# The first matrix of both MLPs by seven products for eight, with the residual kept in DRAM meanwhile

## The chip, the core and the metric

The kernel runs on one core of one Trainium2 chip. The metric is the device time of one execution in microseconds (us); smaller is better. Before the change three runs took 1334.22, 1339.44 and 1339.55 us, with a median of 1339.44 us.

## What is computed

A trunk of two layers over L = 528 tokens (16 meta tokens and 512 tokens of the sequence) with 1024 features, all in float32. Layer 0 mixes tokens by gated DeltaNet heads and windowed attention, layer 1 by dense attention. Behind each mixer stands the same MLP, and it is all that the change touches:

```python
h = h + mix
u = rmsnorm(h, mlp_norm_g[layer])
h = h + jnp.square(jax.nn.relu(u @ w_ff1[layer])) @ w_ff2[layer]   # w_ff1: 1024 x 4096, w_ff2: 4096 x 1024
```

The output is h without the meta tokens, so the mixer's output projection and the MLP of layer 1 work on 512 tokens only.

## The kernel before

Everything stands feature by token: a tile has 128 features on the partitions and the tokens in its columns. The residual is eight such tiles, `hk[0]` to `hk[7]`. A matrix product with full precision is made of three products of a reduced float type: each operand is split into a high part and the rest (`wh` and `wl` of the weights, `xh` and `xl`, or `ah` and `al`, of the activations), and `gemm` (L212) adds wh·xh, wh·xl and wl·xh into one PSUM tile for each of the feature tiles k.

Weights come in units of 1024 by 128 (512 KB). `load_unit` (L201) loads a unit on SyncE's queue into `raw`, ScalarE casts it to `wh` (L208) and VectorE makes `wl` (L209). The three tiles have two buffers each, in the pool `wp`, which is opened first and stays open to the end (L150), so the unit for the next product is prepared while the one before is multiplied, across the borders of stages too. In layer 0 a unit is multiplied with 528 tokens in two halves of 264 columns (48 matmuls); in layer 1 with 512 tokens at once (24 matmuls of 512 columns).

The stages in order: layer 0's mixer (to 348.7 us of the profile), its output projection (O0, L1079 to 1085: eight units; each result is added to the input `hr` by VectorE at L1084, and `make_x` at L1060 and L1061 multiplies with the norm's gain and splits it into `xh` and `xl`), layer 0's MLP (M0), layer 1's mixer with its output projection `c_out` (L1303), and layer 1's MLP (M1).

`mlp` (L1089) goes through the 4096 inner features in four quarters. In each quarter eight units of the first matrix give eight tiles: ScalarE takes relu out of PSUM (L1111), VectorE multiplies with PSUM for the square (L1112), ScalarE casts to `ah` (L1114), VectorE makes `al` (L1115). Then eight units of the second matrix are multiplied with these, and VectorE adds each result to the accumulator `facc` (L1133). The norm's factor is applied last, to the MLP's output: relu(c·u)² is c²·relu(u)², so only `r2` = 1/(mean square + eps) is needed. `sum_squares` (L1065) adds up the squares of `hk`; one matmul with the constant `onesd` (L1122), between the first and the second matrix of the second quarter, sums over the partitions. In the last quarter `facc` is multiplied with `r2` (L1135) and added to `hk` (L1136).

The code is recorded by Python functions; the order in which the instructions stand on each engine is set by a scheduler when the program is built. Each engine works through its own row strictly in that order and waits by semaphores for the others.

Of the kernel before, what the change touches and what calls it, by code (L numbers as in the profile page):

```python
# [17 lines left out]
P = 128  # L18
# [116 lines left out]
def build(tc, ins, out, dbg=None):  # L135
# [891 lines left out]
    ab_cm.__exit__(None, None, None)  # L1027
    psum_pool("psm0", dn=4)
# [49 lines left out]
    xs = []  # L1078
    for m in range(KT):  # L1079
# [5 lines left out]
        xs.append(make_x(m, PK_G + 8))  # L1085
# [3 lines left out]
    def mlp(layer, t0, xs, final):  # L1089
        lp_cm = tc.tile_pool(name=f"mlp{layer}", bufs=1, side="right", reuse_waits="tile")  # L1090
        lp = lp_cm.__enter__()
        acc = lp.tile([P, KT, L], F32, name="facc")
        xh, xl = [x[0] for x in xs], [x[1] for x in xs]
# [313 lines left out]
```

## Time and profile before

| | |
|---|---|
| median of three runs | 1339.44 us |
| the profiled execution's own time | 1335.85 us |
| its span, first to last instruction | 1334.1 us |
| TensorE matmul (PE) busy | 1299.1 us, 97% |
| weight loads (PEld) busy | 1180.8 us, 89% |
| VectorE (DVE), ScalarE (ACT), GpSimd (POOL) busy | 754.9, 558.6, 88.1 us |
| mean granted TensorE clock | 0.991 |
| stages, by the first product of each | O0 from 348.7, M0 from 397.9, M1 from 974.0 us |

The page is read by engine: busy time is the union of an engine's instructions, and an engine's idle time is put down to what ended it. PE's matmuls overlap each other, so how fast PE really goes is read from the distance between two starts and not from a matmul's own length.

### The profile page before, as it was taken

What the parts mean: (1) busy time and instruction counts of PE and PEld (TensorE: products, weight loads), DVE (VectorE), ACT (ScalarE), POOL (GpSimd) and SP (SyncE); (2) the same over time, 40 slices, a digit from 0 to 9 for tenths busy, and PEclk for the clock granted to TensorE, in tenths of its full rate; (3) what the DMA queues carried; (4) which work ended last, traced back from release to release, by engine and by line L of the source; (5) the groups of instructions that cost most, each with busy time, mean ns of one, the idle gap of its engine ahead of it and who ended that gap; (6) DMA issues with size and microseconds to landing.
All of it is one profiled execution on the core that took longest, in us unless ns stands there. A gap on an engine that the chain in (4) does not pass through costs nothing.

```text
span 1334.1 us, 21206 instructions
## 1 busy us (share of the span) xinstructions
PE 1299.1 (97%) x8595; PEld 1180.8 (89%) x8595; DVE 754.9 (57%) x1575; ACT 558.6 (42%) x1084; POOL 88.1 (7%) x202
## 2 busy tenths in 40 slices
PE   7998999899999999999999999999999999999998
PEld 6997999789899999999999987988788888888886
DVE  5686868986554324434335668698663244343444
ACT  4634565556533323223123357576443232231331
POOL 1051506030000000000000000000000000000000
PEclk9998999999899999999999999999999999999999
DMA  4321212100143323332332221101243333333333
GB/s 170 113 64 32 65 33 65 48 2 3 49 126 95 96 83 93 95 91 85 95 96 87 88 85 43 56 16 33 71 117 94 98 95 92 95 95 102 95 97 98
DMA packets 32081, 105.20 MB, mean 79 GB/s; under 512 B 3688, under 2 KB 3816, under 8 KB 31856
## 3 DMA queue, kind: packets, MB, share of 16 engines
q1 hardware_dynamic: 31984, 103.86, 25.9%
q8 instruction: 67, 1.10, 0.4%
q14 instruction: 30, 0.25, 0.1%
HBM read 101.73 MB, written 2.11 MB: 78 GB/s over the span
## 4 chain that ended last, share of the span: by engine, by line
PE 88%; DVE 5%; ACT 3%; POOL 2%; issue 1%; DMA 1%; SPq 0%; ACTq 0%; DVEq 0%
PE dn L219 64%; PE cq L219 5%; PE po L1292 2%; PE dn L1265 2%; PE pw L980 1%; PE pw L1286 1%; POOL u L634 1%; DVE cy L429 1%; POOL ut L633 1%; PE po L219 1%; PE rw L735 1%; PE rw L668 1%; PE rw L682 1%; PE pw L464 1%; PE rw L723 1%
## 5 line engine op out<-in xcount | busy, mean ns | idle before, releaser
L208 ACT CAST wh<-raw 128x1024 fp32r<-128x1024 f32 (+1 forms) x186 | 188.3, 1012 | 479.9 <-PE dn L219 416.7
L209 DVE TENSOR_TENSOR wl<-raw,wh 128x1024 fp32r<-128x1024 f32 (+1 forms) x186 | 219.9, 1182 | 254.0 <-ACT wh L208 249.5
L219 PE MATMUL dn<-xh,wh 128*128 128x264 f32 (+1 forms) x1184 | 297.4, 313 | 1.1 <-ACT wh L208 0.9
L219 PE MATMUL dn<-xh,wl 128*128 128x264 f32 (+1 forms) x1184 | 294.4, 312 | 0.0
L219 PE MATMUL dn<-xl,wh 128*128 128x264 f32 (+1 forms) x1184 | 294.3, 310 | 0.0
L219 PE MATMUL dn<-ah,wh 128*128 128x264 f32 (+1 forms) x896 | 232.3, 318 | 0.0
L219 PE MATMUL dn<-ah,wl 128*128 128x264 f32 (+1 forms) x896 | 230.6, 316 | 0.0
L219 PE MATMUL dn<-al,wh 128*128 128x264 f32 (+1 forms) x896 | 229.4, 314 | 0.0
L219 PEld LDWEIGHTS dn<-xl,wh 128*128 128x128 f32 x1184 | 195.7, 191 | 12.1
L219 PEld LDWEIGHTS dn<-xh,wh 128*128 128x128 f32 x1184 | 195.3, 191 | 12.4 <-issue 1.1
L219 PEld LDWEIGHTS dn<-xh,wl 128*128 128x128 f32 x1184 | 194.0, 190 | 11.1 <-issue 0.2
L219 PEld LDWEIGHTS dn<-al,wh 128*128 128x128 f32 x896 | 148.3, 189 | 11.9 <-issue 0.2
L219 PEld LDWEIGHTS dn<-ah,wh 128*128 128x128 f32 x896 | 148.0, 190 | 10.8 <-ACT ah L1051 0.3
L219 PEld LDWEIGHTS dn<-ah,wl 128*128 128x128 f32 x896 | 147.0, 188 | 11.0
L1133 DVE TENSOR_TENSOR facc<-facc,dn 128x528 f32<-128x528 f32 (+1 forms) x48 | 33.3, 693 | 129.8 <-PE dn L219 129.8
L1114 ACT CAST ah<-rl 128x528 fp32r<-128x528 f32 (+1 forms) x64 | 40.1, 627 | 89.3 <-DVE rl L1112 89.3
L1115 DVE TENSOR_TENSOR al<-rl,ah 128x528 fp32r<-128x528 f32 (+1 forms) x64 | 44.8, 701 | 43.2 <-ACT ah L1114 43.0
L1112 DVE TENSOR_TENSOR rl<-rl,dn 128x528 f32<-128x528 f32 (+1 forms) x64 | 44.1, 689 | 0.0
L429 DVE SCALAR_TENSOR_TENSOR cy<-cin,pk,cy 128x526 f32<-128x526 f32 (+1 forms) x48 | 38.2, 797 | 1.3 <-ACT cy L426 1.0
L1111 ACT ACTIVATE rl<-dn 128x528 f32<-128x528 f32 (+1 forms) x64 | 38.2, 597 | 0.0
L633 POOL TENSOR_TENSOR ut<-abc,u 128x150 f32<-128x150 f32 (+14 forms) x60 | 29.8, 497 | 93.8 <-DVE abc L625 89.5
L1224 POOL MEMSET cvt<- 128x128 f32 x2 | 0.4, 204 | 526.2 <-PE pw L457 526.2
(447 smaller groups left out, 1726.9 us busy)
## 6 DMA issues: line engine op xcount, KB each, us to landing
raw<-in_w SPq DMA_DIRECT2D x128, 512.0 KB, 3.6
raw<-in_w_in SPq DMA_DIRECT2D x22, 512.0 KB, 3.7
raw<-in_w_c SPq DMA_DIRECT2D x12, 512.0 KB, 3.6
raw<-in_w_o SPq DMA_DIRECT2D x8, 512.0 KB, 3.7
raw<-in_w_o SPq DMA_DIRECT2D x16, 256.0 KB, 2.7
gcb<-gdram SPq DMA_DIRECT2D x8, 264.0 KB, 4.5
hr<-in_h SPq DMA_DIRECT2D x8, 264.0 KB, 2.7
out<-h SPq DMA_DIRECT2D x8, 256.0 KB, 2.0
```

Of the source, the lines that this page charges most:

```text
L208: S.copy(out=wh, in_=raw)
L209: V.tensor_tensor(out=wl, in0=raw, in1=wh, op=ALU.subtract)
L219: T.matmul(o, a[:, k, :], b[k][:, sl], start=first and k == 0 and i == 0, stop=last and k == n - 1 and i == 2)
L429: V.scalar_tensor_tensor(out=y[:, a:a + n], in0=x[:, b:b + n], scalar=w(j), in1=y[:, a:a + n], op0=ALU.mult, op1=ALU.add)
L633: G.tensor_tensor(out=ut[:, :, :, :n], in0=arow, in1=ucol, op=ALU.mult)
L1111: S.activation(out=tview(rl), in_=pview(ps), func=AF.Relu)
L1112: V.tensor_tensor(out=tview(rl), in0=tview(rl), in1=pview(ps), op=ALU.mult)
L1114: S.copy(out=a[:, t0:], in_=rl[:, t0:])
L1115: V.tensor_tensor(out=b[:, t0:], in0=rl[:, t0:], in1=a[:, t0:], op=ALU.subtract)
L1133: V.tensor_tensor(out=tview(ak), in0=tview(ak), in1=pview(ps), op=ALU.add)
L1265: T.matmul(ps[:, s, :HL], a[:, sl], b[:, s * HL:(s + 1) * HL], start=i == 0, stop=i == 2)
L1292: T.matmul(po, a[:, kc, :], b, start=kc == 0 and i == 0, stop=kc == NC and i == 2)
```

## The change

The first matrix of both MLPs is multiplied by Strassen's scheme in Winograd's form. Two neighbouring units of the first matrix (two output tiles m and m+1) and the two halves of the 1024 input features make a 2 by 2 block matrix; the feature halves and the two halves of the tokens (264 or 256 columns) make the other one. The eight block products become seven, each of 4 feature tiles by 3 split parts, 12 matmuls of 264 columns in layer 0 and of 256 columns in layer 1.

- **Activations.** `Fast.add` replaces `make_x` behind O0 and `c_out`. It makes the seven operands `B11`, `B21`, `B22`, `T1` to `T4` (sums and differences of the blocks, each split into high part and rest) on ScalarE and VectorE.
- **Weights.** `weight_groups` loads two units at a time (1 MB), VectorE makes the sums of blocks in `sums` (L1226, L1228, L1230 of the new file), and each of three and a half groups a pair is split (L1201, L1202). `prepare` keeps a ring of five split groups. The second matrix goes through the same ring.
- **Products.** `pair` runs the seven products in three banks of PSUM. One of them, `pa`, is copied out by ScalarE three times and goes on accumulating each time; these copies and one of `pd` (`e0` to `e3`) are the partial sums that the outputs share. Relu, square and split follow on ScalarE and VectorE; the last product and the second tile of a pair are finished within the next pair.
- **Residual.** `facc` is gone and `hk` itself is the accumulator. The residual is written to DRAM by GpSimd's DMA queue (`park`) and read back twice (`reload`, into the two buffers of `hr`): for the sum of squares in the second quarter, and in the third quarter, where it is added.
- **Pools.** The weight pool is closed and opened again at each border of stages (`weight_pool`), in the room that other pools have left.

```diff
-    wp = ctx.enter_context(tc.tile_pool(name="wp", bufs=2, side="left"))
...
+    def weight_pool(name, bufs=2):
+        if "cm" in wpool:
+            wpool.pop("cm").__exit__(None, None, None)
+        if name is not None:
+            wpool["cm"] = tc.tile_pool(name=name, bufs=bufs, side="left", reuse_waits="tile")
+            wpool["p"] = wpool["cm"].__enter__()
+        return wpool["p"]
...
+        wp = wpool["p"]
...
+    weight_pool(None)
...
+        def add(self, k):
+            t0, n, g = self.t0, self.n, pkc(self.gcol + k)
+            m, i = t0 + n, k % 4
...
+            if k < 4:
+                x = self.temp.tile([P, L], F32, name=f"xf{k}")
+                S.activation(out=x[:, t0:], in_=hk[k][:, t0:], func=AF.Copy, scale=g)
+                self.split("B11", i, a[:, t0:m], b[:, t0:m], x[:, t0:m])
+                self.first[i] = x
+                V.tensor_tensor(out=x[:, t0:m], in0=x[:, t0:m], in1=x[:, m:], op=ALU.subtract)
+                self.split("T1", i, a[:, m:], b[:, m:], x[:, t0:m])
+                return
+            x, hs = self.first.pop(i), hk[k]
+            S.activation(out=a[:, t0:], in_=hs[:, t0:], func=AF.Copy, scale=g)
+            V.scalar_tensor_tensor(out=b[:, t0:], in0=hs[:, t0:], scalar=g, in1=a[:, t0:], op0=ALU.mult, op1=ALU.subtract)
+            self.ops["B21"][i] = (a[:, t0:m], b[:, t0:m])
+            self.ops["B22"][i] = (a[:, m:], b[:, m:])
+            t2, t3, t4 = fresh("t2"), fresh("t3"), fresh("t4")
+            V.scalar_tensor_tensor(out=t2, in0=hs[:, m:], scalar=g, in1=x[:, t0:m], op0=ALU.mult, op1=ALU.add)
+            self.split("T2", i, *part("T2"), t2, -1.0)
+            V.scalar_tensor_tensor(out=t3, in0=hs[:, m:], scalar=g, in1=x[:, m:], op0=ALU.mult, op1=ALU.subtract)
+            self.split("T3", i, *part("T3"), t3)
+            V.scalar_tensor_tensor(out=t4, in0=hs[:, t0:m], scalar=g, in1=t2, op0=ALU.mult, op1=ALU.subtract)
+            self.split("T4", i, *part("T4"), t4, -1.0)
...
-            s = pool.tile([P, L], F32, name="sqk", tag="sqk", bufs=2)
-            S.activation(out=s[:, t0:], in_=hk[k][:, t0:], func=AF.Square)
+            s = pool.tile([P, L], F32, name="sqk", tag=tags[0], bufs=2)
+            x = src(k)
+            t0 = L - x.shape[1]
+            S.activation(out=s[:, t0:], in_=x, func=AF.Square)
...
+    def park(layer, k, t0=0):
+        G.dma_start(out=hdram[layer][:, k, t0:], in_=hk[k][:, t0:])
+    fq_cm = tc.tile_pool(name="fq0", bufs=1, side="left", reuse_waits="tile")
+    fq = fq_cm.__enter__()
+    ft_cm = tc.tile_pool(name="ft0", bufs=1, side="left", reuse_waits="tile")
+    fast = Fast(fq, ft_cm.__enter__(), PK_G + 8, 0)
+    weight_pool("wo0")
...
-        xs.append(make_x(m, PK_G + 8))
+        park(0, m)
+        fast.add(m)
+    weight_pool(None)
+    ft_cm.__exit__(None, None, None)
...
+        def reload(m):
+            o = mp.tile([P, L], F32, name="hr", tag="hr", bufs=2)[:, t0:]
+            G.dma_start(out=o, in_=hdram[layer][:, m, t0:])
+            return o
+        def weight_groups():
+            def split(src):
+                k = src.shape[1]
+                wh = wp.tile([P, KT, P], F32R, name="wh", tag="wh", bufs=RING)
+                wl = wp.tile([P, KT, P], F32R, name="wl", tag="wl", bufs=RING)
+                S.copy(out=wh[:, :k], in_=src)
+                V.tensor_tensor(out=wl[:, :k], in0=src, in1=wh[:, :k], op=ALU.subtract)
...
+            todo = [(w, q * 8 + m) for q in range(4) for w in ("w1", "w2") for m in range(0, 8, 2)]
+            loaded = [load(*todo[0])]
+            for i, (w, m) in enumerate(todo):
+                if i + 1 < len(todo):
+                    loaded.append(load(*todo[i + 1]))
+                raw = loaded.pop(0)
...
+                s = wp.tile([P, 4, 4, P], F32, name="sums", tag="sums", bufs=1)
+                yield split(flat(raw[:, 0:2]))
+                wide4 = lambda t: t.rearrange("p a k m -> p a (k m)")
+                V.tensor_tensor(out=wide4(s[:, 1:3]), in0=wide4(raw)[:, 0:4:3],
+                                in1=wide4(raw[:, 2:3]).to_broadcast([P, 2, 4 * P]), op=ALU.add)
+                V.tensor_tensor(out=s[:, 3], in0=s[:, 2], in1=raw[:, 0], op=ALU.add)
+                yield split(flat(s[:, 2:4]))
+                V.tensor_tensor(out=s[:, 0], in0=s[:, 3], in1=raw[:, 1], op=ALU.add)
+                yield split(flat(s[:, 0:2]))
+                yield split(raw[:, 3])
...
+        def prepare():
+            while len(groups) < RING or len(groups) - RING in used:
+                g = next(source, None)
+                if g is None:
+                    return
+                groups.append(g)
+        def product(o, g, half, name, start):
+            wh, wl = groups[g]
+            for k in range(4):
+                xh, xl = fast.ops[name][k]
+                for i, (a, b) in enumerate(((wh, xh), (wh, xl), (wl, xh))):
+                    T.matmul(o, a[:, half * 4 + k, :], b, start=start and k == 0 and i == 0, stop=k == 3 and i == 2, skip_group_check=not start)
+        def activated(m, c):
+            S.activation(out=c[:, t0:], in_=c[:, t0:], func=AF.Square)
+            a, b = hl_tile(m, False), hl_tile(m, True)
+            S.copy(out=a[:, t0:], in_=c[:, t0:])
+            V.tensor_tensor(out=b[:, t0:], in0=c[:, t0:], in1=a[:, t0:], op=ALU.subtract)
+            return a, b
+        def pair(base, m, before):
+            ps, ps2 = ps_dense(), ps_dense()
+            pa, pb, pd = ps[:, 0, :n], ps[:, 1, :n], ps2[:, 0, :n]
+            c0 = lp.tile([P, L], F32, name="c0", tag="c0", bufs=2)
+            c1 = lp.tile([P, L], F32, name="c1", tag="c1", bufs=2)
+            lo, hi = slice(t0, t0 + n), slice(t0 + n, L)
+            e = [lp.tile([P, HL], F32, name=f"e{i}", tag=f"e{i}")[:, :n] for i in range(4)]
+            prepare()
+            product(pa, base, 0, "B11", True)
+            S.copy(out=e[0], in_=pa)
+            product(pb, base, 1, "B21", True)
+            used.add(base)
+            V.tensor_tensor(out=c0[:, lo], in0=e[0], in1=pb, op=ALU.add)
+            before()
+            prepare()
+            product(pa, base + 1, 1, "T2", False)
+            S.copy(out=e[1], in_=pa)
+            product(pd, base + 1, 0, "T1", True)
+            used.add(base + 1)
+            S.copy(out=e[2], in_=pd)
+            prepare()
+            product(pa, base + 2, 1, "T3", False)
+            S.copy(out=e[3], in_=pa)
+            V.tensor_tensor(out=c1[:, hi], in0=e[3], in1=e[2], op=ALU.add)
+            product(pd, base + 2, 0, "B22", False)
+            used.add(base + 2)
+            S.activation(out=c1[:, hi], in_=c1[:, hi], func=AF.Relu, scale=-1.0)
+            V.tensor_tensor(out=c0[:, hi], in0=e[1], in1=pd, op=ALU.add)
+            S.activation(out=c0[:, t0:], in_=c0[:, t0:], func=AF.Relu)
+            acts[m] = activated(m, c0)
+            def end():
+                prepare()
+                product(pa, base + 3, 0, "T4", False)
+                used.add(base + 3)
+                S.activation(out=c1[:, lo], in_=pa, func=AF.Relu, scale=-1.0)
+                acts[m + 1] = activated(m + 1, c1)
+            return end
         for q in range(4):
...
+            acts = {}
+            end = lambda: None
+            for m in range(0, 8, 2):
+                end = pair(base, m, end)
+                base += 4
+            end()
             if q == 1:
-                sq = sum_squares(lp, t0)
+                sq = sum_squares(lp, reload, ("c0", "c1"))
...
             for m in range(8):
+                prepare()
+                gemm(dst(ps), groups[base], ah, al)
+                used.add(base)
+                base += 1
+                ak = hk[m]
                 if q == 0:
                     S.copy(out=tview(ak), in_=pview(ps))
-                else:
+                elif q < 3:
                     V.tensor_tensor(out=tview(ak), in0=tview(ak), in1=pview(ps), op=ALU.add)
+                if q == 2:
+                    hr = reload(m)
+                    V.tensor_tensor(out=ak[:, t0:], in0=ak[:, t0:], in1=r2[:, t0:], op=ALU.mult)
+                    V.tensor_tensor(out=ak[:, t0:], in0=ak[:, t0:], in1=hr, op=ALU.add)
                 if q == 3:
-                    V.tensor_tensor(out=ak[:, t0:], in0=ak[:, t0:], in1=r2[:, t0:], op=ALU.mult)
-                    V.tensor_tensor(out=hk[m][:, t0:], in0=hk[m][:, t0:], in1=ak[:, t0:], op=ALU.add)
+                    o = lp.tile([P, L], F32, name="last", tag="c0", bufs=2)
+                    V.tensor_tensor(out=tview(o), in0=tview(r2), in1=pview(ps), op=ALU.mult)
+                    V.tensor_tensor(out=ak[:, t0:], in0=ak[:, t0:], in1=o[:, t0:], op=ALU.add)
...
+    weight_pool("wc")
...
-                xs.append(make_x(m, PK_G + 24, NM))
+                park(1, m, NM)
+                fast.add(m)
...
+    cp_cm.__exit__(None, None, None)
+    fq_cm = tc.tile_pool(name="fq1", bufs=1, side="right", reuse_waits="tile")
+    fq = fq_cm.__enter__()
+    ft_cm = tc.tile_pool(name="ft1", bufs=1, side="right", reuse_waits="tile")
+    fast = Fast(fq, ft_cm.__enter__(), PK_G + 24, NM)
     weave((c_out(4, KT), 1))
-    cp_cm.__exit__(None, None, None)
+    ft_cm.__exit__(None, None, None)
```

**TensorE at the end of the first matrix in the second quarter of layer 0.** Before, the squares' matmul (`sqa`, `onesd`) stands there as well:

```order
L219 MATMUL dn<-xh_4689,wl 128x264 x2
L219 MATMUL dn<-xh_4751,wh 128x264 x2
L219 MATMUL dn<-xl_4752,wh 128x264 x2
L219 MATMUL dn<-xh_4751,wl 128x264 x2
L1122 MATMUL dn<-sqa,onesd 128x264 x2
L219 MATMUL dn<-ah_5762,wh 128x264 x2
```

and with the change (`T4h`, `T4l` are an operand of the last product of a pair):

```order
L1250 MATMUL dn<-T4h_4782,wl 128x264
L1250 MATMUL dn<-T4h_4863,wh 128x264
L1250 MATMUL dn<-T4l_4864,wh 128x264
L1250 MATMUL dn<-T4h_4863,wl 128x264
L1313 MATMUL dn<-sqa,onesd 128x264 x2
L232 MATMUL dn<-ah_5995,wh 128x264 x2
```

The squares' matmul has kept its place: ahead of all products of the second matrix in that quarter.

**ScalarE: the squares.** Before, each of the eight squares (L1070) stands in O0, right behind the tile that it squares:

```order
L208 CAST wh<-raw 128x1024
L1060 ACTIVATE xh_4689<-h,pk 128x528
L1070 ACTIVATE sqk<-h 128x528
L208 CAST wh<-raw 128x1024
L1060 ACTIVATE xh_4751<-h,pk 128x528
L1070 ACTIVATE sqk<-h 128x528
```

With the change one square (L1143) stands in the second quarter's third pair, and seven behind its last pair, each of a tile `hr` that was read back:

```order
L1287 ACTIVATE c_6272<-c_6272 128x264
L1289 ACTIVATE c_6271<-c_6271 128x528
L1296 ACTIVATE c_6272<-dn 128x264
L1254 ACTIVATE c_6271<-c_6271 128x528
L1254 ACTIVATE c_6272<-c_6272 128x528
L1256 CAST ah_6399<-c_6271 128x528
L1256 CAST ah_6421<-c_6272 128x528
L1201 CAST wh<-raw 128x1024
L1143 ACTIVATE sqk<-hr 128x528 x7
L1201 CAST wh<-raw 128x1024 x4
```

So the seven squares have moved behind everything that the last pair asks of ScalarE.

**ScalarE at the opening of O0.** Before, the first unit's cast is not among these rows; it was made earlier:

```order
L770 ACTIVATE osb<-osb,ro 16x128
L1051 CAST ah_4227<-yA_80 128x528
L1051 CAST ah_4231<-yA_81 128x528
L1051 CAST ah_4235<-yA_82 128x528
L1051 CAST ah_4239<-yA_83 128x528
L1051 CAST ah_4243<-yB 128x528
L1051 CAST ah_4247<-yB 128x528
L1051 CAST ah_4251<-yB 128x528
L1051 CAST ah_4255<-yB 128x528
L208 CAST wh<-raw 128x1024
L1060 ACTIVATE xh_4317<-h,pk 128x528
```

With the change:

```order
L783 ACTIVATE osb<-osb,ro 16x128
L1067 CAST ah_4230<-yA_80 128x528
L1067 CAST ah_4234<-yA_81 128x528
L1067 CAST ah_4238<-yA_82 128x528
L1067 CAST ah_4242<-yA_83 128x528
L1067 CAST ah_4246<-yB 128x528
L1067 CAST ah_4250<-yB 128x528
L1067 CAST ah_4254<-yB 128x528
L1067 CAST ah_4258<-yB 128x528
L221 CAST wh<-raw 128x1024 x3
L1116 ACTIVATE xf_4332<-h,pk 128x528
```

The casts of O0's first units now all stand behind the eight casts of the mixer's outputs, three of them ahead of the first result.

## Rows read from the trace of the kernel before

**Rows 1.** The page: engines; the chain that ended last, by engine.

```profile
PE 1299.1 (97%) x8595; PEld 1180.8 (89%) x8595; DVE 754.9 (57%) x1575; ACT 558.6 (42%) x1084; POOL 88.1 (7%) x202
...
PE 88%; DVE 5%; ACT 3%; POOL 2%; issue 1%; DMA 1%; SPq 0%; ACTq 0%; DVEq 0%
```

**Rows 2.** PE's waits over the span: total, times, longest.

```profile
PE dn L297 <- ACT sqk L295: 7.3, 1, 7.3
...
PE dn L219 <- ACT wh L208: 0.9, 1, 0.9
```

**Rows 3.** Windows of the two MLPs: length, busy time by engine, granted clock, DMA.

```profile
397.80:770.00 372.20, 371.49 (x3078) 371.14 (x3077) 157.43 (x178) 114.94 (x146) 0.00 (x0) 1.00 0.31 91
974.00:1329.00 355.00, 354.96 (x1539) 288.46 (x1537) 149.16 (x172) 106.98 (x137) 0.00 (x0) 1.00 0.32 97
```

**Rows 4.** Timeline of PE, layer 0: start, length, instruction; 23 rows between.

```profile
449.95 0.40 PE L219 MATMUL dn<-ah,wh 128*128 128x264 f32 x2
...
455.74 0.40 PE L219 MATMUL dn<-ah,wh 128*128 128x264 f32 x2
```

**Rows 5.** Timeline of PE, layer 1; 26 rows between.

```profile
1039.66 0.40 PE L219 MATMUL dn<-ah,wl 128*128 128x512 f32 x1
...
1045.90 0.40 PE L219 MATMUL dn<-ah,wl 128*128 128x512 f32 x1
```

**Rows 6.** Groups of instructions, 400 to 755 us: count, busy, mean ns, idle before.

```profile
L219 PEld LDWEIGHTS dn<-xl,wh 128*128 128x128 f32 x506 | 78.5, 188 | 0.0
...
L209 DVE TENSOR_TENSOR wl<-raw,wh 128x1024 fp32r<-128x1024 f32 x62 | 75.9, 1224 | 124.9 <-ACT wh L208 120.7 <-PE dn L1122 2.5
...
L208 ACT CAST wh<-raw 128x1024 fp32r<-128x1024 f32 x61 | 64.0, 1049 | 191.0 <-PE dn L219 183.2 <-issue 7.8
L1115 DVE TENSOR_TENSOR al<-rl,ah 128x528 fp32r<-128x528 f32 x32 | 22.7, 708 | 21.8 <-ACT ah L1114 21.7
...
L1114 ACT CAST ah<-rl 128x528 fp32r<-128x528 f32 x32 | 20.3, 634 | 44.7 <-DVE rl L1112 44.7
L1111 ACT ACTIVATE rl<-dn 128x528 f32<-128x528 f32 x32 | 19.3, 604 | 0.0
```

**Rows 7.** Groups of VectorE over the span, smaller forms.

```profile
L209 DVE TENSOR_TENSOR wl<-raw,wh 128x512 fp32r<-128x512 f32 x16 | 10.9, 683 | 0.0
...
L592 DVE TENSOR_TENSOR dt<-pw,dt 128x256 f32<-128x256 f32 x16 | 6.1, 413 | 0.0
```

**Rows 8.** ScalarE out of PSUM, 264 columns: ns min/median/max.

```profile
L319 ACT COPY gt<-rw x2: 368/368/369, 23.4 to 27.2; 32x264 f32<-32x264 f32 x2
```

**Rows 9.** DMA issues: count, KB each, median us to landing.

```profile
raw<-in_w SPq DMA_DIRECT2D x128, 512.0 KB, 3.6
...
hr<-in_h SPq DMA_DIRECT2D x8, 264.0 KB, 2.7
out<-h SPq DMA_DIRECT2D x8, 256.0 KB, 2.0
...
yB<-in_h SPq DMA_DIRECT2D x4, 264.0 KB, 5.7
```

**Rows 10.** Timeline of ScalarE and PE where O0 opens.

```profile
350.20 2.23 ACT L1051 CAST ah<-yB 128x528 fp32r<-128x528 f32 x4
...
348.75 1.46 PE L219 MATMUL dn<-ah,wh 128*128 128x264 f32 x4
```

**Rows 11.** Windows of PE: length, PE busy, granted clock, DMA; three are slow stretches.

```profile
105.00:115.20 10.20, 9.23 (x43) 0.50 0.19 51
347.40:354.20 6.80, 6.75 (x27) 0.50 0.00 1
354.20:360.00 5.80, 5.80 (x49) 1.00 0.10 15
787.70:791.10 3.40, 3.40 (x18) 0.50 0.00 0
```

**Rows 12.** Timeline of PE, the longest wait of the mixer.

```profile
105.97 0.47 PE L659 MATMUL rw<-ident,U 128*128 128x128 f32 x1 [6.06 <-DVE U L646]
```

More of the change, by code (lines that the diff above doesn't have):

```diff
@@ L1047, in build @@
     hk = [h[:, k, :] for k in range(KT)]
+    hdram = [dp.tile([P, KT, L], F32, name=f"hdram{i}") for i in range(2)]
     yh, yl = [], []
@@ L1063, in make_x, with __init__, split @@
         return a, b
-    def sum_squares(pool, t0=0):
+    class Fast:
+        def __init__(self, pool, temp, gcol, t0):
+            self.pool, self.temp, self.gcol, self.t0, self.n = pool, temp, gcol, t0, (L - t0) // 2
+            self.first, self.ops = {}, {n: [None] * 4 for n in ("B11", "B21", "B22", "T1", "T2", "T3", "T4")}
+        def split(self, name, i, a, b, src, sign=1.0):
+            S.activation(out=a, in_=src, func=AF.Copy, scale=sign)
+            if sign == 1.0:
+                V.tensor_tensor(out=b, in0=src, in1=a, op=ALU.subtract)
+            else:
+                V.scalar_tensor_tensor(out=b, in0=src, scalar=sign, in1=a, op0=ALU.mult, op1=ALU.subtract)
+            self.ops[name][i] = (a, b)
+        def add(self, k):
+            t0, n, g = self.t0, self.n, pkc(self.gcol + k)
+            m, i = t0 + n, k % 4
+            a = xp.tile([P, L], F32R, name=f"xh{k}", tag=f"xh{k}")
+            b = xp.tile([P, L], F32R, name=f"xl{k}", tag=f"xl{k}")
+            fresh = lambda name: self.temp.tile([P, HL], F32, name=name, tag=name, bufs=2)[:, :n]
+            part = lambda name: [self.pool.tile([P, HL], F32R, name=f"{name}{c}{i}")[:, :n] for c in "hl"]
+            if k < 4:
[18 more added lines that the diff above has]
+            self.split("T4", i, *part("T4"), t4, -1.0)
@@ new lines, in weight_groups, with load @@
+        def weight_groups():
[5 more added lines that the diff above has]
+                V.tensor_tensor(out=wl[:, :k], in0=src, in1=wh[:, :k], op=ALU.subtract)
+                return wh, wl
+            def load(name, i):
+                raw = wp.tile([P, 4, 4, P], F32, name="raw", tag="raw", bufs=2)
+                for j in range(2):
+                    nc.sync.dma_start(out=raw[:, 2 * j:2 * j + 2].rearrange("p a k m -> p (a k) m"),
+                                      in_=ins[f"{name}_{layer}"][i + j])
+                return raw
+            flat = lambda t: t.rearrange("p a k m -> p (a k) m")
+            todo = [(w, q * 8 + m) for q in range(4) for w in ("w1", "w2") for m in range(0, 8, 2)]
[4 more added lines that the diff above has]
+                raw = loaded.pop(0)
+                if w == "w2":
+                    yield split(flat(raw[:, 0:2]))
+                    yield split(flat(raw[:, 2:4]))
+                    continue
+                s = wp.tile([P, 4, 4, P], F32, name="sums", tag="sums", bufs=1)
+                yield split(flat(raw[:, 0:2]))
+                wide4 = lambda t: t.rearrange("p a k m -> p a (k m)")
[6 more added lines that the diff above has]
+                yield split(raw[:, 3])
@@ L1141, in build @@
     xs2 = []
[L1142 removed]
+    mlp(0, 0, fast, lambda m: xs2.append(make_x(m, PK_G + 16)))
+    weight_pool(None)
+    fq_cm.__exit__(None, None, None)
     tap("h2", h)
@@ L1328, in build @@
     mark("M1")
-    mlp(1, NM, xs, lambda m: nc.sync.dma_start(out=out[m], in_=hk[m][:, NM:]))
+    mlp(1, NM, fast, lambda m: nc.sync.dma_start(out=out[m], in_=hk[m][:, NM:]))
+    weight_pool(None)
+    fq_cm.__exit__(None, None, None)
     psum_pool(None)
```

37 lines of the change are left out of this document (14 added, 23 removed).

## The prediction

> **What bounds the kernel now.** I read the page first: TensorE (PE) is busy in 97% of the span and holds 88% of the chain that ended last [rows 1], so time is saved only where PE has less to do, and lost wherever it is made to wait. Next the list of PE's waits: the longest are 7.3 us at the start and 6.1 us in layer 0's mixer, and all matmuls of L219 together waited 0.9 us for a weight cast [rows 2]. Then the two MLPs by windows: in 372.2 and 355.0 us PE is idle for less than 1 us each, while VectorE (DVE) is busy in 157.4 and 149.2 us and ScalarE (ACT) in 114.9 and 107.0 us [rows 3]. So both MLPs run at PE's pace, with more than half of each other engine free.
>
> PE's pace is read from starts. In layer 0, 48 matmuls of 264 columns lie between 449.95 and 455.74 us: 0.1206 us each [rows 4]. In layer 1, 27 matmuls of 512 columns lie between 1039.66 and 1045.90 us: 0.2311 us each [rows 5].
>
> **What PE saves.** A pair of tiles needs 84 matmuls for 96 in layer 0. Over 16 pairs that is 192 fewer at 0.1206 us, 23.2 us. In layer 1 a pair takes 84 of 256 columns for 48 of 512. No row has 256 columns with these operands; scaled from 264 columns it is 0.117 us. So 1344 at 0.117 us are 157.2 us, where 768 at 0.2311 us were 177.5: 20.3 us saved. Together **-43.5 us**.
>
> This needs each weight load to go on beside another matmul, now with 0.117 us to hide in. A load takes 188 ns [rows 6], yet layer 0 of the kernel before starts a matmul with a load of its own every 0.1206 us [rows 4], so loads overlap there already. The Trainium skill ("TensorE: Matmul & The Clock Gate", the part on packing small matmuls) says that a weight load overlaps with matmuls in flight only where the row groups differ, and these use all rows; it speaks against halving the columns of layer 1. By that rule each of the 1344 would cost its load as well, 0.188 us, and the sum would be 253 us higher; the trace disagrees, with 0.1206 us.
>
> **The squares: the largest cost.** The matmul with `onesd` stands on PE ahead of all products of the second matrix in the second quarter, before and after. Before, its eight squares had been made in O0. Now seven of them stand on ACT behind the last pair's work, and each reads a tile that GpSimd's queue brings back from DRAM into one of two buffers. From the end of the last product the chain goes: ACT's relu of 264 columns (0.37 [rows 8]), two squares (0.60 each, as the relu of 528 in [rows 6]), two casts (0.63 each), one weight cast (1.05) and the second residual's square (0.60): 4.5 us. The third tile has been loaded by then, so three rounds remain in which the other buffer is filled and squared: 3 x (L + 0.65), with L the time from issue to landing and 0.05 for the hand-overs. DVE's last sum (0.70) and its hand-over end it, 0.9. PE has nothing else in its row: it waits 7.4 + 3L.
>
> The trace has no DMA issued by GpSimd. SyncE's load of the same 264 KB lands in 2.7 us, a store in 2.0, one in a crowded queue in 5.7 [rows 9]; these are my bounds, and a faster landing is excluded by the 2.0 of a plain store. I take L = 3.5, near the 2.7, since nothing else is loading much then but GpSimd has to issue it. That gives 17.9 us (13.4 to 24.5), in both layers: **+35.8 us** (27 to 49). The Trainium skill ("DMA: Bandwidth & Descriptors", the anatomy of a DMA on the GpSimd path) gives about 2.0 us plus the bytes at 436 GB/s, an estimate of 2.6 us here; by it the two stalls would be 5.4 us shorter, and no run here shows it yet.
>
> **The openings.** With the weight pool closed at each border, no unit is ready when a stage begins.
> - O0: the first cast now stands behind eight casts which end at 352.43 us (350.20 + 2.23 [rows 10]); with its 1.05 us PE starts at 353.5 instead of 348.75. The rest `wl` of 1.22 us is half covered by the first products: **+5.2 us** (3 to 8).
> - M0: the first pair's load needs the room of `Fast`'s temporaries, so it starts after the last tile's add (0.7) and about 1.1 us of `Fast.add`; it lands in 3.6 us [rows 9] and is cast in 1.05: 6.7 us with hand-overs. Then the second group needs three sums on DVE (1.22 + 2 x 0.68 [rows 6, 7]) and a cast; the first product covers part of it, 3.5 us remain. **+10.2 us** (6.7 to 15).
> - M1: the last tiles of `c_out` have 12 matmuls (2.8 us) each, but the add and `Fast.add` cost DVE 2 x 0.71 + 6 x 0.41 [rows 6, 7], 3.9 us: four tiles lose 4.5. The opening costs M0's 10.2 less the 5.1 by which its load is free earlier, about two tiles. **+9.6 us** (5 to 15).
>
> **Inside a pair** PE has 10.1 us of matmuls. DVE has, in mean durations, 3 x 1.22 + 0.68 for the splits, 1.22 + 2 x 0.68 for the sums, 3 x 0.41 and 2 x 0.71 for the outputs: 9.6 us [rows 6, 7]. ACT has 3.5 x 1.05 for the casts, six of 264 columns at 0.37 and five of 528 at about 0.62: 9.0 us [rows 6, 8]. Back to back they overlap a little (four casts of 0.63 take 2.22 [rows 10]), so both fit, at nine tenths. I take 0.45 us lost a pair, 32 times: **+14 us** (0 to 30), nearer to nothing because the ring of five groups evens it out.
>
> **Clock.** Around 347.4 us, after a stretch in which PE was partly idle, the granted clock was 0.50 (1.2 GHz) for 6.8 us, and later for 3.4 us [rows 11]; PE did 27 matmuls in the first of them, where 49 fit into 5.8 us afterwards. Beside the mixer's 6.06 us wait [rows 12] a slow stretch lasts 10.2 us [rows 11]. Half of a slow stretch is lost: 1.7, 3.4 or up to 5.1 us. Both stalls at the squares are longer than that wait; I take 2.7 us each, between the two shorter ones. The openings of M0 and M1 may cost one more, 1.7: **+7 us** (3 to 12). **The end** loses one of two DVE steps behind the last product: -0.7.
>
> Hidden, at nothing: the parking of `h` and the third quarter's reads (DVE adds 2 x 0.7 us there to a unit of 5.8 us; cover of over 2 us, and if it went, eight waits of L at most); the larger loads (the DMA share is 0.31 [rows 3] and falls).
>
> **Sum:** -43.5 + 35.8 + 5.2 + 10.2 + 9.6 + 14 + 7 - 0.7 = +37.6 us. On the profiled execution's 1335.85 us that is 1373.5, given as **1374 us**. That execution was 3.6 us under the median of three, 1339.44. All low bounds together give 1336, all high ones 1420; the terms are independent of each other, so I take 1350 to 1400 for this case.
>
> **Rivals.**
> 1. *The squares hide* (not slower). All of the reads depend only on two buffers and on squares that ACT could make during the first matrix, whose quarter lasts over 40 us: eight reads of 3.5 us fit. If ACT were through with them 18 us before the last product, 35.8 us and some 4 of the clock go: 1334 us, 1320 to 1345 by the pairs' bounds. It is decided by the place of the seven squares on ACT, and the order shown has them last. Chance 0.07.
> 2. *DVE becomes the bound in the pairs.* DVE waited 0.68 us (21.7 in 32) before each `al` for ACT [rows 6]. If three such waits a pair are not covered, a pair takes 9.6 + 2.0 = 11.6 us, 1.5 lost instead of 0.45: 34 us more, 1408 us. It decides when DVE's row runs behind the ring. Chance 0.13.
> 3. *The scheme does not save on PE:* if a matmul cannot start sooner than 188 ns after another because of its load [rows 6], layer 1 takes 1344 x 0.188 = 252.7 instead of 157.2, and the time is 1469. Layer 0's spacing speaks against it [rows 4]. Chance 0.02.
>
> **Numbers.** The forecast has 0.78. A measurement of this kernel can tell about 0.5%, 6.7 us, from no change: 1333 to 1346. Rival 1 gives half of its chance to faster; a few hundredths of the forecast's low tail lie below 1346. Faster 0.04, same 0.06, slower 0.90. The range goes from 1347 to 1406: it leaves out rivals 1 and 3, half of rival 2 and the forecast's tails, about 0.2.
>
> **What will show it.** The first matrix of a quarter falls from 46.3 us (384 x 0.1206) to about 42.3 (336 x 0.1206, and 4 x 0.45) in layer 0, matmuls of 256 columns start every 0.117 us; PE waits near 18 us for DVE's `sqa` at L1313, twice, with the clock at 0.50 behind it; waits of some us where O0, M0 and M1 begin; a few tenths a pair. The forecast is wrong if L1313 waits under 8 us, if the pairs lose over 1 us each, or if the spacing is not 0.117 us.

## The result, and the profile after

The changed kernel takes 1380.24 us (median of four runs, 1378.83 to 1382.18), the kernel before 1336.83 us in the runs beside it. The ratio is 1.0326, with a 95% interval of 1.0293 to 1.0359: slower. The prediction was 1374 us, in a range of 1347 to 1406. The profiled execution has a span of 1377.1 us, 43.0 more than before; the sum had said 37.6.

The page of the changed kernel, the two lines that answer to [rows 1]:

```profile
PE 1288.0 (94%) x8979; PEld 1188.1 (86%) x8979; DVE 921.8 (67%) x1847; ACT 702.0 (51%) x1412; POOL 113.7 (8%) x250
...
PE 63%; issue 24%; DVE 5%; ACT 4%; POOL 2%; DMA 2%; SPq 0%; POOLq 0%; ACTq 0%; DVEq 0%
```

TensorE is busy for 11.1 us less, yet the span is longer: it waits. The list of its waits names where (the five largest new ones; compare [rows 2]; `po` is a result of `c_out`):

```profile
PE dn L1313 <- DVE sqa L1146: 33.6, 2, 16.9
PE dn L1250 <- ACT wh L1201: 10.9, 3, 6.5
...
PE dn L232 <- ACT wh L221: 4.9, 1, 4.9
PE po L232 <- DVE wl L222: 3.2, 1, 3.2
...
PE dn L1250 <- DVE wl L1202: 1.6, 3, 0.7
```

The squares' matmul alone makes 33.6 us, in two waits. How one of them is built shows in the timeline of layer 0, by engine:

```profile
548.18 0.28 PE L1250 MATMUL dn<-T4h,wl 128*128 128x264 f32 x1
565.35 2.13 PE L1313 MATMUL dn<-sqa,onesd 128*128 128x264 f32 x4 [16.88 <-DVE sqa L1146]
...
549.02 1.16 ACT L1254 ACTIVATE c<-c 128x528 f32<-128x528 f32 x2
550.08 1.15 ACT L1256 CAST ah<-c 128x528 fp32r<-128x528 f32 x2
551.14 1.04 ACT L1201 CAST wh<-raw 128x1024 fp32r<-128x1024 f32 x1
552.09 0.64 ACT L1143 ACTIVATE sqk<-hr 128x528 f32<-128x528 f32 x1
554.09 0.64 ACT L1143 ACTIVATE sqk<-hr 128x528 f32<-128x528 f32 x1 [1.36 <-DVE sqa L1146]
556.12 0.65 ACT L1143 ACTIVATE sqk<-hr 128x528 f32<-128x528 f32 x1 [1.38 <-DMA hr<-hdram]
...
563.91 0.64 ACT L1143 ACTIVATE sqk<-hr 128x528 f32<-128x528 f32 x1 [1.40 <-DMA hr<-hdram]
...
553.02 0.55 POOL L1191 DMA_DIRECT2D hr<-hdram  x1 [7.75 <-ACT sqk L1143]
```

ScalarE gets to the first of the seven squares at 552.09, after relu, squares, two casts and one weight cast. From then on a square comes every 2 us: it frees one of two buffers, GpSimd issues the next read (553.02), and its tile is squared 3.1 us later (556.12). The DMA part of the page gives the landing itself, and shows that the second layer does the same:

```profile
hr<-hdram POOLq DMA_DIRECT2D x16, 264.0 KB, 3.0
...
hr<-hdram POOLq DMA_DIRECT2D x16, 256.0 KB, 2.9
```

The clock is the next cost. Windows of TensorE: in the wait, behind it, and then; and at the openings of M0 and O0 (length, busy, granted clock, DMA share):

```profile
551.00:565.30 14.30, 0.00 (x0) 0.50 0.55 176
565.30:571.40 6.10, 6.05 (x23) 0.50 0.16 47
571.40:580.00 8.60, 8.60 (x73) 1.00 0.20 53
407.63:421.29 13.66, 8.29 (x32) 0.50 0.58 197
349.61:359.85 10.24, 4.87 (x20) 0.50 0.24 69
```

At 0.50 (1.2 GHz) the 6.1 us behind the wait do the work of three: 3.05 us lost. Behind the second wait, in layer 1, the slow stretch lasts 6.0 us, with about the same loss.

What the pairs save is read from the windows of undisturbed quarters, from the first product to the second matrix's first matmul: the last two quarters of layer 0 and of layer 1.

```profile
615.49:658.08 42.59, 42.59 (x338) 41.61 (x337) 31.26 (x41) 31.43 (x55) 0.00 (x0) 1.00 0.29 100
704.38:747.01 42.63, 42.63 (x339) 41.59 (x338) 32.49 (x43) 31.44 (x55) 0.00 (x0) 1.00 0.30 104
1200.71:1242.24 41.53, 41.53 (x338) 40.35 (x336) 30.92 (x41) 30.81 (x55) 0.00 (x0) 1.00 0.30 103
1286.42:1327.97 41.55, 41.55 (x337) 40.34 (x336) 32.12 (x43) 30.84 (x55) 0.00 (x0) 1.00 0.32 106
```

VectorE and ScalarE are busy for three quarters of the time in these windows, so neither is full. Before, the first matrix of a quarter took 384 x 0.1206 = 46.3 us in layer 0 [rows 4] and, by the starts in the trace, 44.4 us in the first two quarters of layer 1 (192 x 0.2311 [rows 5]) and 44.2 in its last two. The change gains 3.7 us a quarter in layer 0 and 2.6 to 2.8 in layer 1, about 25.6 us in eight quarters.

### The profile page after: what moved, and what is told of

Read it like the earlier page. It is cut to its first block, busy times and chain, and to the rows that moved or that the text cites. A ratio compares the mean times of both kernels' runs of the same rounds, so it can differ in the third digit from the quotient of the medians.

```text
span 1377.1 us, 22737 instructions
## 1 busy us (share of the span) xinstructions
PE 1288.0 (94%) x8979; PEld 1188.1 (86%) x8979; DVE 921.8 (67%) x1847; ACT 702.0 (51%) x1412; POOL 113.7 (8%) x250
## 4 chain that ended last, share of the span: by engine, by line
PE 63%; issue 24%; DVE 5%; ACT 4%; POOL 2%; DMA 2%; SPq 0%; POOLq 0%; ACTq 0%; DVEq 0%
PE dn L232 28%; PE dn L1250 12%; PE cq L232 5%; PE po L1495 2%; PE dn L1468 2%; DMA hr<-hdram 1%; PE pw L1489 1%; PE pw L993 1%; POOL u L647 1%; DVE cy L442 1%; PE rw L695 1%; POOL ut L646 1%; PE rw L681 1%; PE rw L748 1%; PE rw L736 1%
## 5 line engine op out<-in xcount | busy, mean ns | idle before, releaser
L1201 ACT CAST wh<-raw 128x1024 fp32r<-128x1024 f32 (+1 forms) x128 | 120.5, 943 | 201.1 <-PE dn L232 172.1
L1202 DVE TENSOR_TENSOR wl<-raw,wh 128x1024 fp32r<-128x1024 f32 (+1 forms) x128 | 139.3, 1090 | 63.9 <-ACT wh L1201 62.2
L1250 PE MATMUL dn<-xh,wh 128*128 128x264 f32 (+1 forms) x512 | 152.6, 298 | 11.7 <-ACT wh L1201 10.9
L1250 PE MATMUL dn<-xh,wl 128*128 128x264 f32 (+1 forms) x512 | 146.8, 289 | 1.6 <-DVE wl L1202 1.6
L1250 PE MATMUL dn<-xl,wh 128*128 128x264 f32 (+1 forms) x512 | 147.2, 288 | 0.0
L1250 PEld LDWEIGHTS dn<-xh,wh 128*128 128x128 f32 x512 | 99.2, 194 | 18.1 <-ACT wh L1201 12.1
L1202 DVE TENSOR_TENSOR wl<-sums,wh 128x1024 fp32r<-128x1024 f32 x64 | 78.0, 1224 | 39.4 <-ACT wh L1201 38.8
L1201 ACT CAST wh<-sums 128x1024 fp32r<-128x1024 f32 x64 | 66.8, 1050 | 72.4 <-PE dn L232 45.2
L1250 PEld LDWEIGHTS dn<-xh,wl 128*128 128x128 f32 x512 | 98.9, 194 | 2.5 <-DVE wl L1202 2.5
L1250 PEld LDWEIGHTS dn<-xl,wh 128*128 128x128 f32 x512 | 99.4, 194 | 0.1
L232 PE MATMUL dn<-xh,wh 128*128 128x264 f32 x416 | 91.5, 297 | 1.1 <-DVE last L1335 0.8
L232 PE MATMUL dn<-xl,wh 128*128 128x264 f32 x416 | 90.4, 293 | 0.0
L232 PE MATMUL dn<-xh,wl 128*128 128x264 f32 x416 | 89.2, 293 | 0.0
L222 DVE TENSOR_TENSOR wl<-raw,wh 128x1024 fp32r<-128x1024 f32 (+1 forms) x58 | 63.0, 1088 | 11.6 <-ACT wh L221 11.1
```

What stands on the lines that cost most here:

```text
L222: V.tensor_tensor(out=wl, in0=raw, in1=wh, op=ALU.subtract)
L232: T.matmul(o, a[:, k, :], b[k][:, sl], start=first and k == 0 and i == 0, stop=last and k == n - 1 and i == 2)
L1201: S.copy(out=wh[:, :k], in_=src)
L1202: V.tensor_tensor(out=wl[:, :k], in0=src, in1=wh[:, :k], op=ALU.subtract)
L1250: T.matmul(o, a[:, half * 4 + k, :], b, start=start and k == 0 and i == 0, stop=k == 3 and i == 2, skip_group_check=not start)
```

## The experiments

Each kernel ran beside the kernel before on the same chip. Ratios are to the kernel before, with 95% intervals; the changed kernel stands at 1.0326.

### 1. The squares later

```diff
-            if q == 1:
-                sq = sum_squares(lp, reload, ("c0", "c1"))
...
             for m in range(8):
                 ps = ps_dense()
...
                     final(m)
+            if q == 1:
+                sq = sum_squares(lp, reload, ("c0", "c1"))
...
```

> The squares, their sums and the matmul with onesd are recorded behind the second matrix of the second quarter instead of ahead of it; r2 is first read in the third quarter. Theory (the changed kernel loses two waits of 16.9 and 16.7 us there, and about 3 us more behind each at a granted clock of 0.50): the two waits fall under 2 us each, the slow stretches behind them go, and the time falls by about 39 us, from 1380 to 1341. Rival A (the wait itself is the whole cost, the clock costs nothing): 34 us less, 1346. Rival B (the squares only push the weight casts back on ScalarE, so the second matrix waits in their place): less than 20 us gained, over 1360, with waits on wh at the second matrix's first units.

Measured: 1342.31 us, 1.0052 (1.0037 to 1.0067), 37.9 us less than the changed kernel. The list of TensorE's waits has none at the squares' matmul any more, and the clock stays at 1.00 from 423.5 to 979.9 us. The quarter behind the moved matmul got 1.0 us longer in layer 0 and 1.3 in layer 1. So 33.6 us of waits and 2 x 3.05 of clock go, 2.3 come back: 37.4. The theory stands, 1 us off; rival B falls, and rival A, which leaves the clock out, is 4 us off.

### 2. Four buffers for the reads

```diff
-            o = mp.tile([P, L], F32, name="hr", tag="hr", bufs=2)[:, t0:]
+            p, tag = (lp, "hs") if m % 2 else (mp, "hr")
+            o = p.tile([P, L], F32, name="hr", tag=tag, bufs=2)[:, t0:]
```

> The reads of the parked residual get four buffers instead of two; nothing else is changed. Theory (the chain of the wait is made of rounds in which a buffer is squared and read again, 2 us a tile, because only two are free): with four buffers, four tiles have landed when ScalarE is through with the last pair, and the remaining three land together; each wait at the squares' matmul falls from 16.9 to about 10.5 us and the time by about 13 us, to 1367 (1362 to 1372). Rival (ScalarE's own work and GpSimd's issuing make the chain, not the number of buffers): each wait stays over 15 us and the time within 4 us of 1380.

Measured: 1369.19 us, 1.0247 (1.0223 to 1.0271), 11.1 us less. The waits in this kernel:

```profile
PE dn L1314 <- DVE sqa L1146: 23.5, 2, 11.8
```

5.1 us less each. The theory had 6.4: the additions to the sum keep ScalarE from squaring the landed tiles back to back, as in this row of its timeline:

```profile
553.67 1.18 ACT L1143 ACTIVATE sqk<-hr 128x528 f32<-128x528 f32 x2 [1.37 <-DVE sqa L1146]
```

The rounds through two buffers were a third of the wait. In layer 0 the first of the seven squares starts 3.6 us after the last product, in both kernels; from there to the end of the sum it is 8.2 us instead of 13.2.

### 3. The openings

```diff
+    unit0 = load_unit(ins["w_o0"][0])
...
+        with tc.issue_after(cast0):
+            S.copy(out=a, in_=s)
...
+        if m == 6:
+            early.append(load_pair(rawp, "w1", 0, 0))
...
+            if k1 == KT and m == 5:
+                early.append(load_pair(rawp, "w1", 1, 0))
```

`rawp` is a pool of two raw tiles, opened ahead of `Fast`'s; `cast0` is the cast of `unit0`.

> Only the openings are changed: the first unit of the output projection is cast ahead of the eight casts of the mixer's outputs, and the raw tiles of the MLP have a pool of their own, so that the first pair's load of each MLP goes out while the output projection still runs. Theory (a stage waits at its start for a load or a cast that comes late): O0's wait of 4.9 us goes, of M0's 6.5, 0.6 and 1.1 us some 3 to 4 go, and M1's opening gets 2 to 4 us shorter; with the clock behind them 8 to 20 us less, about 1368. Rival (the openings wait for the operands that Fast.add makes of the last tile, whatever the weights do): only O0's 4 to 5 us are gained, 1375 or more.

Measured: 1375.16 us, 1.0293 (1.0270 to 1.0315), 5.1 us less: outside the theory's range and, by the number, where the rival has it. The traces divide it, the theory holding at M0 and not at M1: O0's waits at its opening fell from 5.5 to 2.2 us; from O0's first product to the second matrix of M0's first quarter it is 100.6 instead of 105.2 us. M1's first quarter got longer, from 46.3 to 50.1 us, and its start, counted from the statistics of layer 1's mixer, only 1.1 us earlier. The timelines of ScalarE and VectorE there say why:

```profile
990.90 1.03 ACT L1218 CAST wh<-raw 128x1024 fp32r<-128x1024 f32 x1
...
994.32 0.42 DVE L1114 SCALAR_TENSOR_TENSOR T2l<-t,T2h 128x256 fp32r<-128x256 f32 x1
994.65 0.42 DVE L1112 TENSOR_TENSOR T3l<-t,T3h 128x256 fp32r<-128x256 f32 x1
994.99 0.48 DVE L1144 SCALAR_TENSOR_TENSOR t<-h,pk,t 128x256 f32<-128x256 f32 x1
995.39 1.22 DVE L1219 TENSOR_TENSOR wl<-raw,wh 128x1024 fp32r<-128x1024 f32 x1
```

VectorE's rows have no idle time ahead of them: it is full with `Fast.add`, and the first pair's `wl`, whose cast had ended at 991.93, has to queue behind it. TensorE's longest wait for a `wl` there was 3.9 us. Experiment 9 tests this.

### 4. The weight sums on GpSimd

```diff
-                V.tensor_tensor(out=wide4(s[:, 1:3]), in0=wide4(raw)[:, 0:4:3],
+                G.tensor_tensor(out=wide4(s[:, 1:3]), in0=wide4(raw)[:, 0:4:3],
```

The two smaller sums are moved in the same way.

> The three sums of weight blocks of each pair are made by GpSimd instead of VectorE, which takes 2.6 us of its 9.6 us a pair off VectorE. Rival of the prediction (VectorE's row is what the pairs wait for): the first matrix of a quarter falls from 42.4 and 41.4 us towards 40.5 and 39.3, up to 2 us in each of eight quarters, 1364 to 1370. Theory (the pairs lose some 0.5 us by short waits where a product begins, on either engine, and VectorE has time left): no gain, the quarters stay within 0.5 us of 42.4 and 41.4 and the time at 1378 or more; if GpSimd takes over 3 us for the large sum, its row comes late and the time is longer, by up to 2 us a pair, 1440 at the most.

Measured: 1392.33 us, 1.0429 (1.0412 to 1.0446), 12.1 us more. The undisturbed quarters got 0.5 to 0.8 us longer (43.2 and 42.3), the first quarters of M0 and M1 6.0 and 6.3. So nothing was gained, as the theory had it, but the quarters lost more than its 0.5 us. The groups of this kernel, GpSimd's sum and a split on VectorE that was not changed:

```profile
L1226 POOL TENSOR_TENSOR sums<-raw 128x1024 f32<-128x1024 f32 x32 | 84.1, 2627 | 310.8 <-DVE wl L1202 202.9 <-DMA raw<-in_w 107.9
...
L1202 DVE TENSOR_TENSOR wl<-raw,wh 128x512 fp32r<-128x512 f32 x32 | 43.1, 1346 | 10.4 <-ACT wh L1201 8.5
```

In the changed kernel that split takes 688 ns. So the work taken off VectorE came back as slower work of its own, and this run does not show what a freer VectorE would do. The Trainium skill ("SBUF — State Buffer", the section on who interferes with whom) says that a VectorE instruction with two inputs in SBUF contends with a GpSimd instruction that reads SBUF; this split has two such inputs, and 1346 for 688 ns agrees.

### 5 and 6. What the pairs wait for

Both stand on experiment 1. In the first the matmuls of the products keep the order of the code:

```diff
-                    T.matmul(o, a[:, half * 4 + k, :], b, ...)
+                    tc.keep_in_program_order(T.matmul(o, a[:, half * 4 + k, :], b, ...))
```

> On top of e1_mean_late (1342 us): the matmuls of the seven products are pinned to the order in which pair records them; before, TensorE's row has the product T3 in the middle of T1, one matmul behind the copy of pa that it needs. Theory (the 2.1 us that a quarter loses against 336 times 0.1206 us are short waits of a product's first matmul on ScalarE or VectorE, each of which costs some 0.25 us since the next weight load cannot go ahead of it): most of the loss of T3 goes, the quarters of the first matrix fall by 0.5 to 1 us each, from 42.5 and 41.5 to about 41.7 and 40.7, and the time by 4 to 8 us, to 1336. Rival (the engines beside are simply too slow for the pairs, whatever the order): the quarters stay within 0.3 us and the time within 2 us of 1342.

In the second `pa`, `pb` and `pd` are tiles of their own:

```diff
-            ps, ps2 = ps_dense(), ps_dense()
-            pa, pb, pd = ps[:, 0, :n], ps[:, 1, :n], ps2[:, 0, :n]
+            pa, pb, pd = (ps1(tag)[:, :n] for tag in ("pa", "pb", "pd"))
...
-    psum_pool("psm1", dn=4)
+    psum_pool("psm1", dn=2, pa=2, pb=1, pd=1)
```

> On top of e1_mean_late (1342 us): pa, pb and pd are three PSUM tiles of their own (pa with two buffers) and the second matrix keeps two; before, pa and pb are two halves of one tile and the product into pb waits for ScalarE's copy of pa. With it the scheduler writes each product whole, too. Theory (short waits make the pairs' loss): the wait of the product into pb goes as well, the quarters of the first matrix fall by 1 to 1.7 us each, to 41.2 and 40.1, and the time by 8 to 13 us, to about 1331, below the kernel before. Rival (VectorE or ScalarE set the pairs' pace): the waits move to the next product, less than 3 us gained.

Measured: the pinned order 1375.37 us, 1.0285 (1.0269 to 1.0301), 33 us slower than experiment 1 and outside both expectations. Its waits, and one of them in the timeline:

```profile
PE dn L1250 <- ACT e L1270: 21.2, 32, 3.1
...
PE dn L1250 <- DVE c L1273: 9.5, 8, 2.6
...
620.13 0.39 PE L1250 MATMUL dn<-xh,wh 128*128 128x264 f32 x1 [0.54 <-ACT e L1270]
```

L1270 is the copy `e0` of `pa`. The product that waits for it goes into `pb` and needs no copy; it shares a tile with `pa`, and the semaphores are set by the tile. In the code's order it stands right behind the product into `pa`, so it waits in each of 32 pairs. L1273 is the sum that reads `pb`; the product that waits for it, in the first pair of each quarter, goes on in `pa` and doesn't need it either. The scheduler's own order had filled most of that time with matmuls of other products.

With tiles of their own the time is 1328.67 us, 0.9946 (0.9933 to 0.9958): 13.6 us less than experiment 1 and faster than the kernel before. Its third and fourth quarters:

```profile
592.84:634.46 41.62, 41.62 (x338) 41.38 (x337) 34.40 (x43) 31.21 (x55) 0.00 (x0) 1.00 0.30 102
680.77:722.17 41.40, 41.40 (x338) 41.20 (x337) 32.20 (x43) 31.90 (x55) 0.00 (x0) 1.00 0.32 110
1152.01:1192.72 40.71, 40.71 (x338) 40.13 (x337) 34.00 (x43) 30.80 (x55) 0.00 (x0) 1.00 0.32 104
1236.90:1277.23 40.33, 40.33 (x337) 39.99 (x336) 31.66 (x43) 31.29 (x55) 0.00 (x0) 1.00 0.31 109
```

41.4 and 40.3 us in the fourth quarters, where experiment 1 has 42.6 and 41.6, with VectorE and ScalarE as busy as in the changed kernel. So the rival falls. The starts of TensorE say the same: in the changed kernel's window from 615.49 to 658.08 us 15 matmuls start over 0.04 us later than 0.1206 us after the one before, 1.6 us together; in this kernel's from 680.77 to 722.17 four do, 0.4 us together. The pairs' loss was for the most part short waits through a shared tile and through the order that works around it; it was not an engine at its limit. No run has separate tiles in the old order, so these two are not told apart.

Not all of the 13.6 us is the pairs'. The first quarters of M0 and M1 got 3.1 us shorter each, and there the clock differs as well: in the slow stretches at the two openings TensorE was busy for 18.4 us in experiment 1 and for 10.2 here, and half of the difference, some 4 us, is the clock's.

### 7 and 8. The parts together

Experiment 7 is 1 and 3 together. Experiment 8 is 6 with the openings of O0 and M0 as in 3, and M1's as in the changed kernel.

> e1_mean_late and e3_open together. If the two parts add up (38 and 5 us against the changed kernel), 1337 us, the same as the kernel before within 0.5%. If the wait at the squares and the openings share the cost of the clock, up to 3 us more.

> e6_tiles, with the openings of O0 and of M0 as in e3_open and M1's opening left as it was (there e3_open lost 2.6 us, as VectorE's row of Fast.add was the bound). Theory: the parts add up, -38 of the squares, -3.2 and -4.5 of the two openings, -8 to -13 of the pairs, 1320 to 1327, faster than both kernels by 0.6 to 1.2%. Rival (the pairs are bound by another engine): 1332 to 1336, no faster than the kernel before.

Measured: 1335.52 us, 0.9998 (0.9983 to 1.0013), and 1324.16 us, 0.9909 (0.9896 to 0.9923). The parts add up in the first. In the second the pairs gave 13.6 us and the two openings 4.5, for 8 to 13 and 7.7 in the expectation; the sum is in its range. The second takes 0.9% less than the kernel before and 4.1% less than the changed one, with the same seven products.

### 9. VectorE at the end of the output projections

```diff
-            V.scalar_tensor_tensor(out=b[:, t0:], in0=hs[:, t0:], scalar=g, in1=a[:, t0:], op0=ALU.mult, op1=ALU.subtract)
-            self.ops["B21"][i] = (a[:, t0:m], b[:, t0:m])
+            self.ops["B21"][i] = (a[:, t0:m], a[:, t0:m])
...
+            if name in ("T2", "T3", "T4"):
+                b = a
```

> e8_best, and Fast.add leaves out the rests of B21, B22, T2, T3 and T4 (the products take the high part in their place): VectorE has four steps fewer, about 2.0 us, in each of the four last tiles of either output projection; nothing else is left out. Theory (the end of layer 1's output projection and M1's opening go at VectorE's pace, with the operands of Fast.add): PE's wait of 3.3 us on wl in the output projection goes, that of 3.3 us on wh at M1's first product gets 1 to 2 us shorter, the first quarter of M1 falls from 44.7 to about 43, and with half of M0's opening the time falls by 8 to 12 us, to 1312 to 1316. Rival (the openings wait for the weights' loads and casts): less than 3 us gained, over 1321.

Measured in one run: 1313.37 us, 10.8 less than experiment 8; but 4.0 us of this lie ahead of O0 (first product at 350.0 instead of 354.0), which the edit doesn't touch, so it is worth some 7, a little less than expected; it leaves the rests out, so this is a test and not a faster version of the kernel. From the statistics of layer 1's mixer to M1's first product it is 195.5 instead of 200.1 us, M1's first quarter takes 42.7 instead of 44.7, and the 3.3 us wait on `wl` in `c_out` is gone. M0 starts 1.2 us sooner after O0. The waits of experiment 8, and of this run:

```profile
PE pa L1261 <- ACT wh L1218: 8.2, 2, 4.9
...
PE po L232 <- DVE wl L221: 3.3, 1, 3.3
```

```profile
PE pa L1262 <- ACT wh L1219: 7.1, 2, 3.6
```

So the end of `c_out` does go at VectorE's pace, and M1 starts 4.6 us earlier with it. Of M1's opening only a part does: the wait on `wh` at its first product was to get 1 to 2 us shorter and did not (3.5 us for 3.3), and of the 2.0 us that the first quarter gained some 1.2 are the clock's, since TensorE was busy for 3.4 us in the slow stretch there instead of 5.8.

## Why the prediction was right, point by point

| term | forecast, us | measured in the profile, us |
|---|---|---|
| what PE saves, less what the pairs lose | -43.5 + 14 = -29.5 | 4 x 3.7 + 4 x 2.7: -25.6 |
| waits at the squares | +35.8 | +33.6 |
| clock behind them | +5.4 of the 7 | 2 x 3.05: +6.1 |
| O0 and M0 | +5.2, +10.2, 1.6 of the clock: +17.0 | O0 starts 5.6 later, M0 7.5 more, its first quarter is 5.9 longer: +19.0 |
| M1 | +9.6 | start, counted from the second matrix of M0's last quarter, 5.5 later, first quarter 4.8 longer: +10.3 |
| end | -0.7 | -0.4 |
| sum | +37.6 | +43.0 (as the span) |

- **The squares** were right in size and in make. L was taken as 3.5 us and is 3.0, 2.9 in layer 1; 7.4 + 3 x 3.0 gives 16.4, and the wait was 16.9. The estimate of 2.6 us that the prediction took from the Trainium skill ("DMA: Bandwidth & Descriptors") is 0.4 us below the row. Experiment 1 shows that the whole cost hangs on where the matmul that needs them stands, experiment 2 what part the buffers have.
- **The saving on PE** holds: layer 1 starts a matmul of 256 columns every 0.118 us, each with a load of its own. From the first row to the second of the changed kernel are 24 matmuls:

```profile
1300.73 0.28 PE L1250 MATMUL dn<-T2l,wh 128*128 128x256 f32 x1
...
1303.56 0.28 PE L1250 MATMUL dn<-T3h,wl 128*128 128x256 f32 x1
```

  Rival 3 is out, and so, for these loads, is the rule that it was weighed with (the Trainium skill, "TensorE: Matmul & The Clock Gate", the part on packing small matmuls).
- **The pairs** lost some 2 us a quarter: 42.6 less 336 x 0.1206 = 40.5, and 41.5 less 336 x 0.118 = 39.6. That is 0.5 us a pair for a forecast of 0.45. The size was right by luck, since the reason given, that two engines at nine tenths cover each other imperfectly, was not: in the windows above they are busy for three quarters of the time, and experiment 6 takes 0.3 us a pair away with no work taken off either engine. What the last 0.2 us a pair are was not looked into. Rival 2 needed a VectorE whose row is longer than the pair, and it falls with the same windows.
- **The openings** came out near their sum by two errors that cancel. The waits were over-sized: at M0's first groups TensorE waited 8.5 us (6.45 + 0.45 + 1.10 + 0.45) for a forecast of 10.2, by the chain that was described (load, cast, sums, cast); at M1 it waited 3.2 us for `wl` in `c_out` and 4.8 at the first products, 8.0 for a forecast of 9.6. The clock was the term most under-sized: a slow stretch of 13.7 us lies over M0's opening and one as long over M1's, and half of what TensorE did in them is lost, 8.29 / 2 and 9.16 / 2, 8.7 us where the prediction had 1.6 left for both. O0 had a slow stretch before as well [rows 11] and lost nothing more by it. The waits at M0's first groups, and M1's window in the form of those above:

```profile
410.99 0.59 PE L1250 MATMUL dn<-xh,wh 128*128 128x264 f32 x1 [6.45 <-ACT wh L1201]
412.25 0.59 PE L1250 MATMUL dn<-xh,wl 128*128 128x264 f32 x1 [0.45 <-DVE wl L1202]
415.93 0.59 PE L1250 MATMUL dn<-xh,wh 128*128 128x264 f32 x1 [1.10 <-ACT wh L1201]
417.19 0.59 PE L1250 MATMUL dn<-xh,wl 128*128 128x264 f32 x1 [0.45 <-DVE wl L1202]
```

```profile
998.14:1011.79 13.65, 9.16 (x34) 0.50 0.49 178
```

## What to carry to other kernels

A saving on the bounding engine is worth only what its row lets through: here some 26 us were saved, and one matmul whose operands were made too late took 40 back, at an unchanged place in TensorE's row. When an operand moves from made early to read back late, look for the latest place at which its result is needed and move the reader there; it cost one moved block. Before a wait in a pipeline is put down to a slow engine, look which semaphore ends it: a tile shared by two unrelated results makes waits that no data asks for.

## What the runs showed of the hardware beyond that

A wait on a matmul costs more than its length. Starts of TensorE in a pair of the changed kernel:

```profile
619.62 0.28 PE L1250 MATMUL dn<-xh,wl 128*128 128x264 f32 x1
619.89 0.39 PE L1250 MATMUL dn<-T2h,wh 128*128 128x264 f32 x1
620.12 0.28 PE L1250 MATMUL dn<-T2l,wh 128*128 128x264 f32 x1
620.24 0.28 PE L1250 MATMUL dn<-T2h,wl 128*128 128x264 f32 x1
```

The matmul at 619.89 waits for a sum of VectorE (L1273, through the shared tile) that ends at 619.83. It starts 0.27 us after the one before, 0.15 later than in the stream, and the next one 0.23 us after it, 0.11 late once more: 0.26 us for a matmul that was 0.15 late. The weight loads of these two matmuls:

```profile
619.89 0.19 PEld L1250 LDWEIGHTS dn<-T2h,wh 128*128 128x128 f32 x1 [0.20 <-DVE c L1273]
620.00 0.19 PEld L1250 LDWEIGHTS dn<-T2l,wh 128*128 128x128 f32 x1
```

In the stream a load starts 0.12 us ahead of its matmul. The waiting matmul's load started only with it, at 619.89, and the next load 0.11 us behind, so its matmul was late as well. I read the loss from this; no run tests it by itself. Such steps don't appear in the list of waits, which counts none in this quarter; they are seen only in the distance between starts.
